# One encoder layer with forgetting attention, RWKV-7 and product-key experts: VectorE in source order in the recurrent part of the second half

## The chip, the core and the metric

The kernel is one program on one core of a Trainium2 chip. The metric is device time in microseconds (us): from the start of the program on the core to its end, median of several executions. Engines are named as the profile names them: PE (TensorE) multiplies matrices, DVE (VectorE) and POOL (GpSimd) do elementwise work, ACT (ScalarE) does activations and copies, SP (SyncE) only issues DMAs. Every engine works through its own queue in the order in which the program was laid out, and an instruction whose inputs are not there yet holds up everything behind it on that engine.

## What is computed

One layer, batch 1, 1024 tokens, width 1024, float32: a combined projection, two token-mixing branches (forgetting attention and RWKV-7), a gated merge with a LayerNorm, and then a product-key mixture of single-neuron experts (PEER) with another LayerNorm. Cut to what matters here:

```python
# branch B, RWKV-7, 8 heads x 64: a recurrence over the tokens
def frame_step(state, inp):
    r_t, w_t, k_t, v_t, kk_t, a_t = inp
    sa = jnp.einsum('bhij,bhj->bhi', state, -kk_t)
    state = (state * w_t[:, :, None, :] + sa[..., None] * (kk_t * a_t)[:, :, None, :]
             + v_t[..., None] * k_t[:, :, None, :])
    return state, jnp.einsum('bhij,bhj->bhi', state, r_t)
# then a group norm per head, a bonus term, and a product with the output gate g

# PEER, per block of 128 tokens xb, 8 heads, 16 experts per head and token
q = (xb @ w_q).reshape(t, 8, 2, 128)
s = jnp.einsum('thpd,hpkd->thpk', q, sub_keys)       # scores against 2 x 128 keys
top_s, top_i = lax.top_k(s, 16)                      # and top 16 of the 256 pair sums: idx, gate
h = jax.nn.gelu(jnp.einsum('thkd,td->thk', u_table[idx], xb))   # gathered rows of u, dot products
return jnp.einsum('thk,thkd->td', gate * h, v_table[idx])
```

## The kernel before

The 1024 tokens go through the front part in two halves of 512 (the loop over `PARTS` in `body`). Each half runs attention (`fox`), then the recurrent branch (`rwkv_half`), then the merge, the first LayerNorm and the expert queries (`merge_half`). After both halves `dense_block` does the experts: three of the eight blocks of 128 tokens as dense products, five by gathered rows.

**Background work.** As soon as the first half has its scores, the experts of its tokens are started beside the second half's front part. This is the queue `g.B` (class `Background`, line 156): for block after block it holds `topk` (line 1266, DVE: maxima, indices, one-hot sums) mixed with `experts_in` (line 1376). `experts_in` gathers, for each of 128 expert slots, one row of the table `u` per token: an indirect DMA that POOL issues (L1389) into one of `GBUF` = 5 buffers `g`; three slots later a DVE instruction (L1394, here called a dot product) multiplies the rows with the tokens `ext` and sums them into a column of `hh`. When the 128 slots of a block are done, a table of gates is loaded, a Gelu and a product follow (L1399 to L1402), and the next block loads its indices (`eidx`, L1380) into the same buffer and starts over. `Background.tick` (line 182) is called by `mm` (line 276) for every matrix product with the product's planned time; the time is added to a credit, and while the credit is positive one step of the queue is written into the program (a dot product counts 1.46 us of credit). So the place of the background work in the source follows the products: so many dot products per us of planned PE time.

**Order.** The program's order on each engine is made when it is built. PE is under a manual schedule (`MANUAL`, line 58): it follows the source. The other engines are ordered by a planner that takes, at every step, the instruction that is first in the source among those whose inputs it believes to be ready. On DVE it may thus set a background instruction ahead of an operation of the recurrence, or the other way round; on the chip the order is then fixed.

**The recurrent part.** `rwkv_half` (line 722) first makes projections (`shifted`, line 750: 24 products, an ACT copy, two DVE instructions L756, L757), then four times `unit(ct)` (line 900), one for each pair of heads. A unit first makes `M` (L918), then inverts a triangular matrix in six levels of three steps, each step a group of products followed by one DVE operation on their result: `x` (L942), `Tm` (L952), `V` (L958); then `At` (L993) and `Q` (L999), and last a loop over the 8 chunks of 64 tokens that carries the state `sigma` (L1010: copied from PSUM by DVE and ACT by turns). Between the steps `wait(...)` (line 904) writes filler work into the source, from a queue `F`: the elementwise preparation `elem` of the next unit (line 819) and projections for the gates (line 760). A group norm and the output gate follow (L1052 to L1080).

**Weights.** Each block of weights `wraw` is split into a high part `wh` (ACT) and a low part `wl` (L295): POOL makes `wl`, except for every eighth block (`g.lo_mod` = 8, line 320), where DVE does.

Of the kernel before, what the change touches and what calls it, by code (L numbers as in the profile page):

```python
# [155 lines left out]
class Background:  # L156


    def __init__(self, tc):
        self.tc = tc  # L160
        self.q, self.done, self.credit, self.rate, self.busy = [], set(), 0.0, 1.0, False
        self.other = None

    def add(self, gen, *tags):
        self.q.append((gen, tags))
# [16 lines left out]
    def tick(self, us):  # L182
        if self.busy or not self.q or (self.other and self.other.busy):
            return
        self.busy = True
        self.credit += us * self.rate
        while self.q and self.credit > 0:
            c = self._step()
            if c is None:
                self.credit = 0.0  # L190
                break
            self.credit -= c
        self.busy = False
# [185 lines left out]
def body(ctx, g):  # L379
# [61 lines left out]
    with ExitStack() as fe:  # L441
        g.X = None
        front_setup(g, fe, order)
        for hf, (t0, n) in enumerate(PARTS):
            g.t0, g.n, g.cols = t0, n, slice(t0, t0 + n)
            with ExitStack() as hx:
                hp = hx.enter_context(tc.tile_pool(name="hp", bufs=1))
                kt = hp.tile([128, 4, n], F32, name="kt")
                if g.X is None:
                    xload(g, hf)  # L450
                g.B.rate = RATEP[0]
                fox(g, hf, g.X)
                g.B.rate = RATEP[1]
                yr = rwkv_half(g, hf, g.X, kt) if g.stop != "fox" else None
                g.xs.close()
                g.X = None
                g.B.rate = RATEP[2]
                if g.stop not in ("fox", "rwkv"):
                    merge_half(g, hf, yr)
# [262 lines left out]
def rwkv_half(g, hf, X, kt):  # L722
# [12 lines left out]
    with ExitStack() as fx:  # L735
# [164 lines left out]
        def unit(ct):  # L900
# [3 lines left out]
            def wait(us):  # L904
                F.fill(WAIT * us)
# [5 lines left out]
            for u in range(0, NC, 4):  # L911
                us = slice(u, u + 4)
                pm = psM.tile([128, 2, 4, 128], F32, name="pm")
                for c in range(4):
                    for e in range(2):
                        mm(g, pm[:, e, c, :], fl(bk[rows[e], u + c, e:e + 2, :]), fl(arv[rows[e], u + c, 0:2, :]), True, True)
                for e in range(2):
                    dve.tensor_mul(M[:, e, us, :], pm[:, e], tb("m1")[:, None, :].to_broadcast([128, 4, 128]))  # L918
                wait(WT[0])
                pt = psM.tile([128, 2, 8, 64], F32, name="pm")  # L920
                for c in range(4):
# [14 lines left out]
            Tm, Vm = None, None  # L936
            for m in range(6):
                px = psS.tile([128, NC, 64], F32, name="s")
                for e, c in items:
                    mm(g, px[rows[e], c, :], LT(e, c), i64[rows[e]] if Tm is None else Tm[rows[e], c, :], True, True)  # L940
                x = cp.tile([128, NC, 64], F32, name="x")
                dve.tensor_mul(x, px, lev[:, m:m + 1, :].to_broadcast([128, NC, 64]))  # L942
                wait(WT[2])
                if m < 5:
                    Tn = cp.tile([128, NC, 64], F32, name="Tm")
                    if Tm is None:
                        dve.tensor_add(Tn, x, i64b)
                    else:
                        pt = psS.tile([128, NC, 64], F32, name="s")
                        for e, c in items:  # L950
                            mm(g, pt[rows[e], c, :], Vm[rows[e], c, :], x[rows[e], c, :], True, True)
                        dve.tensor_add(Tn, pt, Tm)  # L952
                    Tm = Tn
                pv = psS.tile([128, NC, 64], F32, name="s")
                for e, c in items:
                    mm(g, pv[rows[e], c, :], x[rows[e], c, :], i64[rows[e]] if Vm is None else Vm[rows[e], c, :], True, True)
                Vn = cp.tile([128, NC, 64], F32, name="V")
                dve.tensor_add(Vn, pv, i64b if Vm is None else Vm)  # L958
                Vm = Vn
                wait(WT[3])  # L960
                if m == 1:
# [8 lines left out]
            for u in range(0, NC, 8):  # L970
# [8 lines left out]
                for e in range(2):  # L979
                    r = rows[e]  # L980
                    (dve.tensor_copy if e and not SM & 32 else act.copy)(AV[r, e, us, :], pw[r, :, 64:128])
            wait(WT[5])
            pa = psS.tile([128, NC, 64], F32, name="s")
            for e, c in items:
                r = rows[e]
# [11 lines left out]
                mm(g, pq[r, c, :], W_[r, c, :], M[r, e, c, 0:64], True, True)  # L997
            Q = cp.tile([128, NC, 64], F32, name="x")
            dve.tensor_add(Q, pq, arv[:, :, 0, :])  # L999
            wait(WT[6])  # L1000
            py = psS.tile([128, NC, 64], F32, name="s")
            for c in range(NC):
# [4 lines left out]
                    mm(g, pss[r, :], BK[:, e, c, :], AV[:, e, c, :], True, False)  # L1007
                for r in rows:
                    mm(g, pss[r, :], At[r, c, :], g.sigma[r, ct, par, :], False, True)
                (act.copy if c % 2 or SM & 64 else dve.tensor_copy)(g.sigma[:, ct, 1 - par, :], pss)  # L1010
                for e, r in enumerate(rows):
                    mm(g, py[r, c, :], AV[:, e, c, :], M[:, e, c, 0:64], True, False)
                for r in rows:
# [54 lines left out]
        for ct in range(4):  # L1068
# [8 lines left out]
            b = el.tile([128, n], F32, name=("rt", "vt")[ct % 2])  # L1077
            sp.dma_start(b, g.bvd[ct * 128:(ct + 1) * 128, g.t0:g.t0 + g.n])
            pool.tensor_add(y, y, b)
            dve.tensor_mul(y, y, pgs[ct])  # L1080
            if "yr" in g.dbg:
                sp.dma_start(g.dbg["yr"][ct * 128:(ct + 1) * 128, g.t0:g.t0 + g.n], y)
# [765 lines left out]
```

## Time and profile before

| what | us |
|---|---|
| median of 3 executions (3715.09 to 3723.62) | 3722.64 |
| the profiled execution, its own time | 3689.26 |
| span of the profiled execution | 3687.5 |
| DVE busy in the span | 2366.5 (64%) |
| PE busy in the span | 3232.5 (88%) |
| recurrent part of the second half, 1040 to 1600 us of the span | 560 |
| DVE busy in it | 507.46 |
| PE busy in it | 431.97 |

The profiled execution is one execution, 33.4 us below the median of the others. Busy time counts an instruction from its start to its end, also while it is held up by another engine, so "busy" is not "at its peak". A row of the waits view says which instruction ended an idle stretch of an engine, and how much idle time lay before it.

### The profile page before, as it was taken

To read this page: it belongs to the slowest core of one execution; us is meant where nothing else is said; L and a number is where in the kernel's file an instruction comes from. 1 tells how busy PE (TensorE), PEld (TensorE's weight loads), DVE (VectorE), ACT (ScalarE), POOL (GpSimd) and SP (SyncE) were. 2 spreads that over 40 slices of the span, in tenths; PEclk is the share of its full clock that TensorE was granted. 3 is DMA by queue.
4 is the path that set the end of the run, shared out by engine and by line. 5 is a ranking of instruction groups with operands and counts; after the bars stand their busy time and mean duration, and the time that the engine had idled before them with its cause. 6 is when DMAs were issued, how large, how long until landed. Compare 5 with 4: busy or idle time off the path is not lost. (4 is left out here: it accounts for less than half of the span.)

```text
span 3687.5 us, 55563 instructions
## 1 busy us (share of the span) xinstructions
PE 3232.5 (88%) x20656; PEld 2334.0 (63%) x20656; DVE 2366.5 (64%) x5125; ACT 1241.6 (34%) x2530; POOL 2243.2 (61%) x1752
## 2 busy tenths in 40 slices
PE   7899998989987877667868867899998999999998
PEld 5577777875565656546733322587776777777666
DVE  3235423558889998899669955477665767675324
ACT  3443222333443221222234433333333333333333
POOL 2031115326566556677846566688887888886773
PEclk9999999998888777889989989899999999999999
DMA  4121124548877777877869999899999999999994
GB/s 144 52 92 45 45 96 137 189 140 283 262 262 263 243 233 247 295 259 258 309 245 397 395 343 371 337 364 361 385 383 331 392 398 396 394 396 355 403 394 164
DMA packets 338127, 1019.61 MB, mean 277 GB/s; under 512 B 46272, under 2 KB 84928, under 8 KB 336064
## 3 DMA queue, kind: packets, MB, share of 16 engines
q0 software_dynamic: 184320, 671.17, 49.0%
q1 hardware_dynamic: 141424, 324.11, 24.7%
q10 hardware_dynamic: 12112, 20.78, 1.5%
q8 instruction: 162, 2.65, 0.3%
q14 instruction: 109, 0.89, 0.1%
HBM read 960.81 MB, written 55.12 MB: 276 GB/s over the span
## 5 line engine op out<-in xcount | busy, mean ns | idle before, releaser
L1389 POOL DMA_INDIRECT g<-u,eidx x640 | 789.0, 1233 | 397.1 <-DVE hh L1394 114.5
L1394 DVE CUSTOM_DVE_ANT_0 g<-g,ext 128x1024 f32<-128x1024 f32 x640 | 862.5, 1356 | 165.2 <-DMA g<-u,eidx 164.1
L295 POOL TENSOR_TENSOR wl<-wraw,wh 128x1024 fp32r<-128x1024 f32 x131 | 323.7, 2471 | 503.4 <-ACT wh L294 475.6
L1689 POOL DMA_INDIRECT vr<-v,ve x428 | 458.6, 1072 | 193.0 <-issue 99.9
L277 PE MATMUL pg<-vr,win 128*32 128x512 f32 x1712 | 322.4, 633 | 81.9 <-DMA vr<-v,ve 81.1
L277 PE MATMUL b<-xh,uh 128*128 128x384 f32 x1024 | 352.3, 344 | 22.1 <-DVE C L1574 22.0
L277 PE MATMUL b<-xh,ul 128*128 128x384 f32 x1024 | 348.9, 341 | 1.3 <-POOL ul L295 1.1
L277 PE MATMUL b<-xl,uh 128*128 128x384 f32 x1024 | 348.8, 341 | 0.0
L294 ACT CAST wh<-wraw 128x1024 fp32r<-128x1024 f32 x150 | 157.2, 1048 | 505.1 <-PE pj L277 280.2
L277 PE MATMUL v<-vl,ch 128*128 128x512 f32 x768 | 305.9, 398 | 11.2 <-POOL vl L295 11.1
L277 PE MATMUL pj<-xh,wh 128*128 128x512 f32 x624 | 289.9, 465 | 21.1 <-ACT xh L294 7.9
L277 PE MATMUL v<-vh,ch 128*128 128x512 f32 x768 | 303.3, 395 | 0.0
L277 PE MATMUL v<-vh,cl 128*128 128x512 f32 x768 | 301.4, 392 | 0.0
L1689 POOL DMA_INDIRECT C<-v,ve x212 | 225.6, 1064 | 84.8 <-issue 54.4
L294 ACT CAST uh<-uraw 128x512 fp32r<-128x512 f32 x256 | 158.2, 620 | 350.2 <-PE b L277 322.3
L277 PE MATMUL pj<-xh,wl 128*128 128x512 f32 x624 | 262.2, 420 | 4.3 <-POOL wl L295 2.5
L277 PE MATMUL pj<-xl,wh 128*128 128x512 f32 x624 | 263.1, 422 | 2.2 <-DVE xl L295 2.2
L294 ACT CAST vh<-vraw 128x512 fp32r<-128x512 f32 x256 | 157.7, 620 | 217.7 <-PE v L277 182.9
L277 PEld LDWEIGHTS b<-xh,uh 128*128 128x128 f32 x1024 | 194.1, 190 | 55.7 <-DVE C L1574 26.0
L295 POOL TENSOR_TENSOR ul<-uraw,uh 128x512 fp32r<-128x512 f32 x128 | 168.4, 1316 | 88.3 <-ACT uh L294 86.5
L295 DVE TENSOR_TENSOR vl<-vraw,vh 128x512 fp32r<-128x512 f32 x128 | 130.0, 1016 | 143.0 <-ACT vh L294 136.0
L277 PEld LDWEIGHTS b<-xl,uh 128*128 128x128 f32 x1024 | 194.2, 190 | 14.4 <-issue 10.1
(353 smaller groups left out, 6577.5 us busy)
## 6 DMA issues: line engine op xcount, KB each, us to landing
wraw<-w SPq DMA_DIRECT2D x150, 512.0 KB, 3.4
uraw<-ut SPq DMA_DIRECT2D x128, 512.0 KB, 6.6
vraw<-vt SPq DMA_DIRECT2D x128, 512.0 KB, 7.7
cd<-S SPq DMA_DIRECT2D x12, 1344.0 KB, 10.1
C<-cd SPq DMA_DIRECT2D x63, 256.0 KB, 9.2
g<-u,eidx POOLq DMA_INDIRECT x640
gtd<-tmp ACTq DMA_DIRECT2D x32, 256.0 KB, 4.3
g<-gtd SPq DMA_DIRECT2D x32, 256.0 KB, 3.7
```

The source lines that it names most:

```text
L277: g.pe.matmul(o, l, r, start=start, stop=stop_)
L294: g.act.copy(hi, src)
L295: (lo_eng or g.dve).tensor_sub(lo, src, hi.bitcast(F32))
L1389: pool.indirect_dma_start(out=gg, out_offset=None, in_=A["u"], in_offset=bass.IndirectOffsetOnAxis(ap=idx[:, s_:s_ + 1], axis=0))
L1394: dve.tensor_tensor_reduce(out=gg, in0=gg, in1=xt, scale=1.0, scalar=0.0, op0=OP.mult, op1=OP.add, accum_out=hh[:, k:k + 1])
L1689: g.pool.indirect_dma_start(out=place, out_offset=None, in_=g.A["v"], in_offset=bass.IndirectOffsetOnAxis(ap=self.meta[i][1][:, t:t + 1], ...
```

## The change

`Background` gets `hold` and `release`. While it is held, credit is still added up, but no step is written into the source; at the release the steps that the credit allows are written. `unit` holds it around each group of products up to and including the DVE operation that works on them. For the second half alone, DVE follows the source in all of `rwkv_half`, the state copies all go to ACT, and all low parts of weights go to POOL from there to the end of the half (`g.lo_mod` is not set back). In the group norm the last product with the output gate moves into a loop of its own.

```diff
     def tick(self, us):
         if self.busy or not self.q or (self.other and self.other.busy):
             return
+        self.credit += us * self.rate
+        if self.held:
+            return
         self.busy = True
-        self.credit += us * self.rate
...
+    def hold(self):
+        self.held = True
+    def release(self):
+        self.held = False
+        self.tick(0.0)
...
                 g.B.rate = RATEP[1]
+                if hf:
+                    g.lo_mod = 1000
+                    mans(g, MANUAL | {mybir.EngineType.DVE})
                 yr = rwkv_half(g, hf, g.X, kt) if g.stop != "fox" else None
+                mans(g, MANUAL)
...
                 px = psS.tile([128, NC, 64], F32, name="s")
+                g.B.hold()
                 for e, c in items:
                     mm(g, px[rows[e], c, :], LT(e, c), i64[rows[e]] if Tm is None else Tm[rows[e], c, :], True, True)
                 x = cp.tile([128, NC, 64], F32, name="x")
                 dve.tensor_mul(x, px, lev[:, m:m + 1, :].to_broadcast([128, NC, 64]))
+                g.B.release()
                 wait(WT[2])
...
```

The same pair stands around the products and the operation for `M`, for `Tm`, for `V`, and once around `pa`, `At`, `pq` and `Q` together.

```diff
-                (act.copy if c % 2 or SM & 64 else dve.tensor_copy)(g.sigma[:, ct, 1 - par, :], pss)
+                (act.copy if c % 2 or hf else dve.tensor_copy)(g.sigma[:, ct, 1 - par, :], pss)
...
             pool.tensor_add(y, y, b)
+        for ct in range(4):
+            y = yr[:, ct, :]
             dve.tensor_mul(y, y, pgs[ct])
```

In the first half nothing is in the background queue that could run (its scores are not there yet), so there only the last of these edits has an effect on what is written.

## Rows read from the trace of the kernel before

**Rows 1.** Windows view: stretch, its length, busy time (instructions) of each engine, clock.

```profile
1040.00:1600.00 560.00, 431.97 (x4215) 325.00 (x4214) 507.46 (x1115) 139.61 (x212) 366.74 (x271) 0.81 0.77 260
1142.00:1556.00 414.00, 314.76 (x3770) 238.00 (x3769) 371.40 (x876) 86.13 (x137) 255.68 (x196) 0.79 0.76 257
401.00:468.00 67.00, 62.32 (x924) 48.13 (x924) 30.90 (x52) 18.80 (x31) 11.86 (x8) 0.97 0.13 46
1600.00:1740.00 140.00, 97.99 (x421) 76.16 (x420) 133.53 (x235) 33.14 (x43) 100.60 (x61) 0.92 0.74 249
```

**Rows 2.** Waits of PE, 1142 to 1556 us: us in total, times, longest.

```profile
PE s L277 <- DVE x L942: 38.1, 15, 10.1
PE s L277 <- DVE Tm L952: 17.8, 8, 5.5
PE s L277 <- DVE x L999: 15.7, 4, 6.4
```

**Rows 3.** Waits of DVE, 1040 to 1600 us: us in total, times, longest.

```profile
DVE g L1394 <- DMA g<-u,eidx: 24.5, 23, 2.9
DVE sigma L1010 <- PE s L277: 13.5, 8, 3.8
DVE M L918 <- PE pm L277: 4.1, 4, 1.6
```

**Rows 4.** Groups of DVE, 1040 to 1600 us: count | busy, mean ns | idle before.

```profile
L1394 DVE CUSTOM_DVE_ANT_0 g<-g,ext 128x1024 f32<-128x1024 f32 x217 | 291.1, 1351 | 25.0 <-DMA g<-u,eidx 24.5
L295 DVE TENSOR_TENSOR wl<-wraw,wh 128x1024 fp32r<-128x1024 f32 x4 | 4.9, 1218 | 0.0
L1010 DVE COPY sigma<-s 128x64 f32<-128x64 f32 x16 | 3.5, 221 | 13.5 <-PE s L277 13.5
```

**Rows 5.** Groups of ACT, 1142 to 1556 us, and of POOL, 1040 to 1590 us.

```profile
L294 ACT CAST wh<-wraw 128x1024 fp32r<-128x1024 f32 x18 | 18.9, 1048 | 125.2 <-PE pj L277 121.2 <-DVE tv L1290 4.0
L1010 ACT COPY sigma<-s 128x64 f32<-128x64 f32 x16 | 3.4, 211 | 60.9 <-PE s L277 60.8
L871 ACT ACTIVATE ag<-ag,oka,vec 128x512 f32<-128x512 f32 x3 | 2.4, 813 | 11.7 <-DVE kk L866 11.7
...
L295 POOL TENSOR_TENSOR wl<-wraw,wh 128x1024 fp32r<-128x1024 f32 x26 | 65.6, 2522 | 13.1 <-ACT wh L294 12.7
```

**Rows 6.** Timelines of DVE and PE, 1474 to 1506 us: start, length, instruction [idle before].

```profile
1484.42 1.23 DVE L1394 CUSTOM_DVE_ANT_0 g<-g,ext 128x1024 f32<-128x1024 f32 x1 [2.90 <-DMA g<-u,eidx]
1490.14 0.69 DVE L942 TENSOR_TENSOR x<-s,tab 128x512 f32<-128x512 f32 x1
...
1475.40 1.10 PE L277 MATMUL s<-V,x 64*64 64x64 f32 x32
...
1490.89 1.97 PE L277 MATMUL s<-x,V 64*64 64x64 f32 x32 [10.05 <-DVE x L942]
```

**Rows 7.** Timeline of all engines, 1236 to 1262 us.

```profile
1235.69 4.02 DVE L1394 CUSTOM_DVE_ANT_0 g<-g,ext 128x1024 f32<-128x1024 f32 x1
1236.28 2.35 POOL L295 TENSOR_TENSOR wl<-wraw,wh 128x1024 fp32r<-128x1024 f32 x1
1239.92 0.48 PE L277 MATMUL s<-sigma,Tm 64*64 64x64 f32 x4 [3.57 <-DVE sigma L1010]
```

**Rows 8.** Timelines of SP, POOL and DVE, 1136 to 1161 us: a change of block.

```profile
1145.86 0.32 SPq L1380 DMA_DIRECT2D eidx<-seld  x1
...
1148.61 0.96 POOL L1389 DMA_INDIRECT g<-u,eidx  x1 [8.91 <-DVE ti L1299]
...
1153.54 1.22 DVE L1394 CUSTOM_DVE_ANT_0 g<-g,ext 128x1024 f32<-128x1024 f32 x1 [0.78 <-DMA g<-u,eidx]
```

**Rows 9.** Timeline of all engines, 1552 to 1600 us: the group norm.

```profile
1554.12 0.59 ACT L1016 COPY kt<-s 128x512 f32<-128x512 f32 x1 [0.26 <-PE s L277]
1576.00 0.81 ACT L1074 ACTIVATE kt<-kt,vec 128x512 f32<-128x512 f32 x1 [9.61 <-DVE kt L1072]
1580.61 0.79 PE L277 MATMUL a<-xh,wh 128*128 128x512 f32 x1 [0.78 <-DVE kt L1072]
```

More of the change, by code (lines that the diff above doesn't have):

```diff
@@ L161, in __init__ @@
         self.q, self.done, self.credit, self.rate, self.busy = [], set(), 0.0, 1.0, False
-        self.other = None
+        self.other, self.held = None, False
+    def hold(self):
[3 more added lines that the diff above has]
+        self.tick(0.0)
     def add(self, gen, *tags):
@@ L938, in unit @@
                 px = psS.tile([128, NC, 64], F32, name="s")
+                g.B.hold()
                 for e, c in items:
@@ L942, in unit @@
                 dve.tensor_mul(x, px, lev[:, m:m + 1, :].to_broadcast([128, NC, 64]))
+                g.B.release()
                 wait(WT[2])
@@ L949, in unit @@
                         pt = psS.tile([128, NC, 64], F32, name="s")
+                        g.B.hold()
                         for e, c in items:
@@ L952, in unit @@
                         dve.tensor_add(Tn, pt, Tm)
+                        g.B.release()
                     Tm = Tn
                 pv = psS.tile([128, NC, 64], F32, name="s")
+                g.B.hold()
                 for e, c in items:
@@ L958, in unit @@
                 dve.tensor_add(Vn, pv, i64b if Vm is None else Vm)
+                g.B.release()
                 Vm = Vn
@@ L982, in unit @@
             wait(WT[5])
+            g.B.hold()
             pa = psS.tile([128, NC, 64], F32, name="s")
@@ L999, in unit @@
             dve.tensor_add(Q, pq, arv[:, :, 0, :])
+            g.B.release()
             wait(WT[6])
```

## The prediction

> **What bounds the kernel now.** I read the windows view first, in steps of 20 and 100 us, to find the recurrent part of the second half: 1040 to 1600 us of the span. The reader is to see in its row that DVE, and not PE, is the full engine there [rows 1]: DVE is busy 507.5 of 560 us, PE 432.0. The same unit in the first half, with no background, takes 67 us with DVE at 30.9 [rows 1]; here four units take 414 us, 103 each. So the 36 us more per unit are background work on DVE, and what the stage can win without less work on DVE is at most its idle time, 560 - 507.5 = 52.5 us.
>
> Second, the waits of PE. PE waits for `x` 38.1 us, for `Tm` 17.8, for `Q` (written as tile x, L999) 15.7 [rows 2]. It looks like a chain held up by DVE, and this is what the change goes for. But the waits of DVE say what is behind it: its own idle time is mostly dot products that wait for gathered rows (24.5 us, 23 times), then state copies that wait for PE (13.5), then `M` (4.1) [rows 3]. The timeline of one bad place shows both at once [rows 6]: PE has nothing to do for 10.05 us until `x` is there, `x` starts at 1490.14 behind dot products, and the first of these stood 2.90 us waiting for its rows.
>
> The amount of background work in the stage does not change: credit is still counted per planned product, only its place within a few products moves. So this is a sum over DVE's idle time and over the few operations that change engine.
>
> **The change part by part.** Each term is for the stage, in us against before; the numbers in brackets are its bounds.
>
> 1. *State copies to ACT.* 16 copies of 0.221 leave DVE: -3.5. ACT does them in 0.211 each, and it is busy 86 of 414 us there [rows 1, 4, 5]; a copy that comes behind a weight cast waits up to 1.05 [rows 5]. The 13.5 us in which DVE stood at the head of its queue for a state copy go [rows 3]; dot products pass. Part of it comes back, since the chunk loop is bound by PE and ACT and DVE then meets the next unit's `M` early, where it already waits 4.1. I take two thirds: -9 (0 to -13.5).
>
> 2. *Low parts of weights to POOL.* Four in this stage: -4 x 1.218 = -4.9 on DVE [rows 4], +4 x 2.522 = 10.1 on POOL, which is busy 367 of 560 [rows 1, 5]. But a POOL split holds up DVE: a dot product that met one took 4.02 instead of 1.23 [rows 6, 7], 2.8 more, while an unlucky meeting is not certain (the mean dot product is 1.351 [rows 4]). At 1.5 us for each of the four this gives back 6: net +1 (-4.9 to +6.3). A rule speaks against this edit: the Trainium skill, SBUF — State Buffer, section "Who interferes with whom", has it that a DVE instruction with two SBUF inputs and a GpSimd instruction that reads SBUF exclude each other, and the later one blocks fully. By it and the row the whole split would be lost to DVE, 10.1 against 4.9, and this term would be +5 rather than +1; the row agrees with the blocking. The merge and the queries get the same trade for four more blocks; DVE is busy 133.5 of 140 us at first there [rows 1], and I cost it at 0, covered by POOL's split of a block ahead of its use (-3 to +4).
>
> 3. *Chain operation first, dot products behind it.* PE's waits for `x`, `Tm` and `Q` shrink, but that is time only where DVE was idle too. With the hold, dot products come one to three at a time between operations of the chain instead of in rows, so the gathers (five buffers) run further ahead; and while DVE waits for one, PE already works on the next group. Of the 24.5 us of waits for rows [rows 3], 3.7 stand at the two changes of block (0.78 and 2.90 [rows 6, 8]); of the other 20.8 I take 8: -8 (0 to -14). It cannot be more than a part: the filler behind `x` still brings its own ticks, so the credit of 1.7 us (16 products at 0.107 by the plan) and of 1.6 us of filler puts about two dot products between `x` and `Tm` as before.
>
> 4. *Changes of block in source order.* Here the change adds a wait. The first dot product of a new block is the next background step after the gates' product, and DVE now stands at it: from the load of the indices at 1145.86 over the first gather at 1148.61 to the dot product at 1153.54 are 7.7 us [rows 8]. Behind it on DVE are the chain's operations, and PE waits for these. Before, DVE filled this time with maxima of the next block and idled only 0.78 and 2.90 [rows 6, 8]. Two changes lie in the stage: 2 x 7.7 - 3.7 = 11.7 at most, 0 if the gap in the credit (1.46 per step) and chain operations that come in between cover it; half: +6.
>
> 5. *Preparation in source order.* Each of four `elem` has about three DVE operations directly behind an activation (0.81 [rows 5]): up to 12 x 0.81 = 9.8, 0 where dot products stand ahead of them; half: +5.
>
> 6. *Group norm.* From the last copy at 1554.12 to the first product of the merge at 1580.61 pass 26.5 us, 9.61 of them with ACT waiting for one DVE product that stood behind background work [rows 9]. In source order it stands behind the dot product of two matrix products. The product with the gate in a loop of its own keeps DVE from standing at each POOL addition, which it would otherwise do in source order. -5 (-9.6 to +3).
>
> Sum: -3.5 - 9 + 1 - 8 + 6 + 5 - 5 = -13.5 us. On the profiled execution's 3689.26 that is 3675.8. The sum is a difference, and the median of the runs lies 33.4 us above the profiled execution, so the forecast for the median is 3722.64 - 13.5 = 3709. What is won stays won: behind the stage the source places the same work, and DVE still is full up to 1740 [rows 1].
>
> **The rivals.**
>
> *No change.* DVE was 91% busy and its work stays. A planner that passes over what is not ready keeps an engine fuller than the source order does, so terms 1 and 3 may be eaten by 4 and 5. For it: 507.5 of 560. Against it: 13.5 us for state copies that plainly go. Time: terms 1, 2, 4, 5 alone give -3.5 - 9 + 1 + 6 + 5 = -0.5: 3722.
>
> *Slower.* The dot products at the head of DVE's queue wait for rows, and now nothing passes them. Place: every gather that POOL issues behind a split of 2.5 us [rows 5], and the two changes of block. Price: without terms 3 and 4 the sum is -10.5; waits that grow from 1.07 each (24.5 / 23 [rows 3]) to 2.4 are 55 us, 30.7 more: +20, 3743. It decides for slower from 46 us of such waits on, 2.0 each, since -10.5 + 21.5 = +11. For it: DMAs are late already with the planner's order. Against it: 217 dot products in 560 us are one per 2.6 us, twice their length.
>
> *Much faster.* The idle time of PE breaks into short pieces, and with it the granted clock rises. The row before it: after 10.05 us of idle PE ran 32 products in 1.97 us, against 1.10 without such an idle time [rows 6]; the clock is 0.79 in the units here and 0.97 in the first half's [rows 1], between the two levels 1.2 and 2.4 GHz. PE's busy 314.8 us at 0.79 would be some 20% shorter at 0.97. It counts only where PE holds DVE up, in the chunk loop and the group norm; with all terms at their good bounds -3.5 - 13.5 - 4.9 - 14 - 9.6 = -45.5. Time: some 35 us less, 3688.
>
> *It does not do what it says* (the operations still come behind dot products, by the filler's own ticks) is the first rival's time, since then only DVE's total counts.
>
> **How the numbers follow.** A difference of 0.3%, 11 us, is about what a measurement of this kernel can tell from no change. Forecast (11 to 30 us less, 3693 to 3711): 0.36. Much faster: 0.10. No change: 0.32. Slower: 0.22. So faster 0.46, same 0.32, slower 0.22. The predicted time is the forecast's, 3709. The range goes from 3682, which leaves out half of the much faster case (0.05), to 3740, which leaves out about half of the slower one (0.11).
>
> **What would show it.** Term 1: no state copy on DVE in the second half, and no wait of 13.5 for it; where the 9 us went shows in the wait of `M`. Term 2: dot products of 3 to 4 us beside POOL's splits, their mean above 1.351. Term 3: PE's waits for `x` and `Tm` well below 38.1 and 17.8, DVE's for rows below 24.5. Term 4: two gaps of up to 7.7 us on DVE, each ended by the first gather of a block. Term 5: DVE waits that ACT ends. Term 6: less than 26.5 us from the last copy to the merge's first product. The prediction is wrong if DVE's busy time in the stage is not near 500 us, so that the background work did move, or if the gain of the stage is lost again in the merge.

## The result: 1.3% slower, and the profile after

The changed kernel takes 3768.7 us (median of 4 runs, 3765.01 to 3770.3), the kernel before 3720.95 beside it (3715.09 to 3723.62): a ratio of 1.0130, 95% interval 1.0113 to 1.0147. The forecast was 3709, the range ended at 3740. The profiled execution of the changed kernel spans 3763.2 us.

To lay the two executions side by side I cut them at the same events: the end of attention's last product, the first product of unit 0, the last copy of the recurrent part, the first product of the merge, the first product of the one-hot stage (in `dense_block`, behind both halves). Windows view of the kernel before (stretch, length, busy time and instructions of PE, PEld, DVE, ACT, POOL, then PE's clock, DMA share, GB/s): projections and first preparation, the four units, the whole recurrent stretch up to the merge, the merge and the scores.

```profile
1033.60:1142.80 109.20, 91.53 (x361) 70.01 (x360) 101.27 (x169) 42.77 (x61) 80.80 (x54) 0.89 0.79 268
1142.80:1554.10 411.30, 312.07 (x3764) 237.04 (x3763) 369.25 (x867) 84.13 (x132) 254.74 (x195) 0.79 0.76 257
1033.60:1580.60 547.00, 421.43 (x4183) 315.95 (x4182) 494.10 (x1086) 137.16 (x210) 354.19 (x263) 0.81 0.77 260
1580.60:1872.30 291.70, 219.66 (x979) 175.92 (x979) 224.05 (x373) 72.79 (x103) 202.80 (x126) 0.91 0.75 258
```

The same four stretches of the changed kernel:

```profile
1037.80:1150.20 112.40, 87.99 (x354) 68.00 (x354) 88.18 (x130) 39.90 (x59) 80.10 (x51) 0.86 0.67 221
1150.20:1585.30 435.10, 313.07 (x3764) 238.73 (x3764) 388.38 (x884) 88.96 (x151) 269.68 (x201) 0.79 0.76 251
1037.80:1612.20 574.40, 421.29 (x4177) 318.15 (x4177) 496.90 (x1055) 138.34 (x223) 367.69 (x266) 0.80 0.75 246
1612.20:1910.60 298.40, 224.51 (x980) 180.58 (x980) 230.37 (x380) 73.10 (x105) 209.88 (x130) 0.88 0.75 252
```

Read DVE's column against the length. In the whole stretch DVE has the same work, 494.1 and 496.9 us; what grew is its idle time, from 52.9 to 77.5 us, and the stretch with it, from 547.0 to 574.4. Of the 24.6 us of new idle time 16.3 lie ahead of unit 0 (7.9 became 24.2), 4.7 in the units (42.0 to 46.7), 3.6 in the group norm. Ahead of unit 0 the phase itself is only 3.2 us longer, but 13.1 us of DVE work that used to be done there now lie in the units, whose DVE work grew by 19.1. Behind the merge 6.7 us more follow, 6.3 of them DVE work. Together, from attention's end to the one-hot stage: 838.7 to 872.8, 34.1 us more, with DVE work 718.2 to 727.3 and idle time 120.6 to 145.5. Both kernels do 299 dot products in it, 419.0 and 417.4 us. The rest of the span (1815 us before, 1853 after) does not belong to the change: in repeats of both kernels on another chip it took 1816.0 (e0_before_again) and 1811.5 (e8_after_again).

Waits of DVE in the changed kernel, 1040 to 1612 us (us in total, times, longest), the answer to [rows 3]:

```profile
DVE g L1420 <- DMA g<-u,eidx: 34.4, 24, 8.9
DVE rt L770 <- ACT tmp L768: 6.2, 2, 5.3
DVE M L933 <- PE pm L287: 6.1, 3, 5.3
DVE lora L770 <- ACT tmp L768: 4.0, 1, 4.0
```

The state copies' 13.5 us are gone. Waits for rows grew by 9.9 us with almost the same count: the longest is 8.9 instead of 2.9. The growth lies at the two changes of block (below), not in the other waits for rows. New are operations that wait for ACT. PE's waits in the units, 1150 to 1588 us (answer to [rows 2]), and ahead of them, 1040 to 1150 us:

```profile
PE s L287 <- DVE x L959: 49.7, 18, 11.0
PE s L287 <- DVE Tm L971: 26.9, 8, 6.8
PE pm L939 <- DVE M L933: 19.1, 4, 12.2
PE s L287 <- DVE x L1022: 5.1, 4, 1.3
...
PE pj L287 <- POOL wl L305: 11.6, 1, 11.6
PE s L287 <- ACT tmp L818: 10.8, 2, 8.5
```

PE waits longer for `x` (38.1 before) and `Tm` (17.8), though these now stand ahead of the dot products; only `Q` (15.7 to 5.1) is better off. The groups of DVE, ACT and POOL (answers to [rows 4, 5]):

```profile
L1420 DVE CUSTOM_DVE_ANT_0 g<-g,ext 128x1024 f32<-128x1024 f32 x212 | 285.9, 1365 | 34.5 <-DMA g<-u,eidx 34.4
...
L1034 ACT COPY sigma<-s 128x64 f32<-128x64 f32 x32 | 6.8, 212 | 57.8 <-PE s L287 56.0 <-ACT sigma L1034 1.6
...
L305 POOL TENSOR_TENSOR wl<-wraw,wh 128x1024 fp32r<-128x1024 f32 x30 | 76.4, 2546 | 25.4 <-ACT wh L304 25.1
```

**A change of block** (timelines of SP, POOL, DVE and PE of the changed kernel, 1162 to 1180 us; answer to [rows 8]):

```profile
1164.35 0.33 SPq L1425 DMA_DIRECT2D eidx<-gated  x1
...
1167.60 0.29 DVE L1427 TENSOR_TENSOR hh<-hh,eidx 128x128 f32<-128x128 f32 x1 [1.02 <-DMA eidx<-gated]
...
1167.92 0.32 SPq L1406 DMA_DIRECT2D eidx<-seld  x1
...
1171.42 0.96 POOL L1415 DMA_INDIRECT g<-u,eidx  x1 [9.98 <-DMA eidx<-seld]
...
1175.68 1.22 DVE L1420 CUSTOM_DVE_ANT_0 g<-g,ext 128x1024 f32<-128x1024 f32 x1 [7.79 <-DMA g<-u,eidx]
...
1176.83 1.28 DVE L933 TENSOR_TENSOR M<-pm,tab 128x512 f32<-128x512 f32 x2
...
1178.26 0.37 PE L939 MATMUL pm<-base,bkh 64*128 64x64 f32 x2 [12.23 <-DVE M L933]
```

From the load of the indices at 1167.92 to the dot product at 1175.68 are 7.76 us, as before; but now DVE stands at that dot product for 7.79 us, `M` stands behind it, and PE behind `M` for 12.23. The second change costs 2.31 us for the product with the gates and 8.91 for the first dot product:

```profile
1495.49 0.96 DVE L1427 TENSOR_TENSOR hh<-hh,eidx 128x128 f32<-128x128 f32 x1 [2.31 <-ACT hh L1426]
1505.36 1.23 DVE L1420 CUSTOM_DVE_ANT_0 g<-g,ext 128x1024 f32<-128x1024 f32 x1 [8.91 <-DMA g<-u,eidx]
```

In the kernel before the first dot products of the two blocks waited 0.78 [rows 8] and 1.47 us, and the second ones 2.83 and 2.90 [rows 6]:

```profile
1159.05 1.22 DVE L1394 CUSTOM_DVE_ANT_0 g<-g,ext 128x1024 f32<-128x1024 f32 x1 [2.83 <-DMA g<-u,eidx]
1479.69 1.23 DVE L1394 CUSTOM_DVE_ANT_0 g<-g,ext 128x1024 f32<-128x1024 f32 x1 [1.47 <-DMA g<-u,eidx]
```

In the changed kernel the second ones wait 0 and 0.26. So the first two dot products of the new blocks went from 8.0 to 17.0 us of waiting, and all other waits for rows from 16.5 to 17.4.

**The phase of the projections** (timelines of ACT, POOL and PE of the changed kernel, 1120 to 1137 us):

```profile
1124.28 1.05 ACT L304 CAST wh<-wraw 128x1024 fp32r<-128x1024 f32 x1 [3.79 <-PE pj L287]
...
1124.74 1.75 POOL L1415 DMA_INDIRECT g<-u,eidx  x1 [3.30 <-DVE hh L1420]
1127.84 1.64 POOL L1415 DMA_INDIRECT g<-u,eidx  x1 [1.35 <-DVE hh L1420]
...
1133.97 2.51 POOL L305 TENSOR_TENSOR wl<-wraw,wh 128x1024 fp32r<-128x1024 f32 x1
...
1136.53 0.80 PE L287 MATMUL pj<-xh,wl 128*128 128x512 f32 x1 [11.64 <-POOL wl L305]
```

This one I had not foreseen. The gathers on POOL wait for buffers that late dot products free (`DVE hh`). A low part of weights stands behind five gathers in POOL's queue; ACT had its input ready at 1125.33, POOL starts at 1133.97, and PE has nothing to do for 11.64 us. A late DVE thus comes back to PE over POOL's queue.

### The profile page after: what moved, and what is told of

Read it like the earlier page. It is cut to its first block, busy times and chain, and to the rows that moved or that the text cites. A ratio compares the mean times of both kernels' runs of the same rounds, so it can differ in the third digit from the quotient of the medians.

```text
span 3763.2 us, 55577 instructions
## 1 busy us (share of the span) xinstructions
PE 3236.2 (86%) x20656; PEld 2346.7 (62%) x20656; DVE 2363.6 (63%) x5101; ACT 1240.1 (33%) x2545; POOL 2271.0 (60%) x1760
## 3 DMA queue, kind: packets, MB, share of 16 engines
q0 software_dynamic: 184320, 671.17, 48.6%
q1 hardware_dynamic: 141424, 324.11, 24.6%
## 5 line engine op out<-in xcount | busy, mean ns | idle before, releaser
L305 POOL TENSOR_TENSOR wl<-wraw,wh 128x1024 fp32r<-128x1024 f32 x139 | 343.0, 2467 | 510.4 <-ACT wh L304 484.0
L287 PE MATMUL pg<-vr,win 128*32 128x512 f32 x1712 | 311.2, 646 | 82.4 <-DMA vr<-v,ve 74.3
L287 PEld LDWEIGHTS v<-ab 128*128 128x128 f32 x768 | 113.0, 219 | 167.9 <-issue 103.5
```

The costliest lines, as they stand in the source:

```text
L287: g.pe.matmul(o, l, r, start=start, stop=stop_)
L305: (lo_eng or g.dve).tensor_sub(lo, src, hi.bitcast(F32))
```

## Experiments

Kernels of one group ran on one chip beside the kernel before, which took 3692.49 us (e0 to e3), 3727.05 (e4 to e7), 3693.79 (e8 to e11), 3698.33 (e12 to e15) and 3691.06 (e16, e17). All ratios are to the kernel before on that chip; "stretch" is from attention's end to the merge in the profiled execution, DVE's idle time is its length less DVE's busy time.

| kernel | ratio [95%] | stretch | DVE busy | idle |
|---|---|---|---|---|
| before / after | 1.0130 [1.0113, 1.0147] | 547.0 / 574.4 | 494.1 / 496.9 | 52.9 / 77.5 |
| e0_before_again | 1.0002 [0.9978, 1.0026] | 542.6 | 494.0 | 48.6 |
| e1_planner_order | 1.0023 [1.0002, 1.0045] | 545.7 | 500.2 | 45.5 |
| e2_source_order_alone | 1.0126 [1.0086, 1.0166] | 594.5 | 506.0 | 88.5 |
| e3_from_units | 1.0077 [1.0055, 1.0099] | 569.2 | 490.5 | 78.7 |
| e4_pause | 1.0081 [1.0055, 1.0107] | 586.9 | 501.6 | 85.3 |
| e5_units_pause | 1.0056 [1.0035, 1.0078] | 570.6 | 496.5 | 74.1 |
| e6_sigma_only | 1.0008 [0.9992, 1.0023] | 542.5 | 492.9 | 49.6 |
| e7_no_lo | 1.0012 [0.9995, 1.0029] | 562.0 | 499.7 | 62.3 |
| e8_after_again | 1.0107 [1.0085, 1.0129] | 576.5 | 496.5 | 80.0 |
| e9_prep_only | 1.0065 [1.0040, 1.0089] | 553.2 | 497.3 | 55.9 |
| e10_source_lo8 | 1.0081 [1.0057, 1.0106] | 569.8 | 497.1 | 72.7 |
| e11_units_pause_lo8 | 1.0072 [1.0047, 1.0096] | 570.0 | 499.8 | 70.2 |
| e12_source_no_hold | 1.0113 [1.0087, 1.0140] | 580.7 | 495.5 | 85.2 |
| e13_half_before | 0.9751 [0.9724, 0.9778] | 469.8 | 348.9 | 120.9 |
| e14_half_after | 0.9755 [0.9732, 0.9779] | 510.6 | 386.3 | 124.3 |
| e15_rate | 1.0142 [1.0118, 1.0166] | 498.8 | 452.0 | 46.8 |
| e16_rate_shift | 0.9993 [0.9973, 1.0014] | 492.6 | 450.4 | 42.2 |
| e17_rate_small | 0.9987 [0.9966, 1.0007] | 524.2 | 481.0 | 43.2 |

The idle time is that of one execution: e1 and e7 differ by 16.8 us in it and by 0.1% in the ratio, so a difference of that size in this column decides nothing by itself.

**Which edit: the order or the rest.** First the kernel before unaltered, then the change without its order, then the order alone:

```diff
# e1_planner_order: the changed kernel, less one line
-                    mans(g, MANUAL | {mybir.EngineType.DVE})
# e2_source_order_alone: the kernel before, with that line (and its end) alone
+                if hf:
+                    mans(g, MANUAL | {mybir.EngineType.DVE})
                 yr = rwkv_half(g, hf, g.X, kt) if g.stop != "fox" else None
+                mans(g, MANUAL)
```

> The kernel before, once more, for a second profile of it: the first one (3689 us) lies some 30 us under the other executions. The source-order theory, by which the loss lies in the recurrent part: time 3715 to 3724, and the stretch from the first product of unit 0 in the second half to the end of the queries' scores as in the first profile, 719 us (1142.8 to 1861.7), within 5 us; what the first profile had less than a usual execution lies behind it, in the one-hot part and the experts (1800 us in the first profile, about 1830 here). The rival that part of the loss lies in the experts: this stretch is 1800 us again.

> The changed kernel with one line taken out: DVE stays in the planner's order in the second half. Hold and release, the state copies on ACT, the low parts of weights on POOL and the group norm's second loop stay. Source-order theory: the loss goes, ratio to the kernel before 0.995 to 1.003, PE's waits of 12.2 and 11.6 us at the change of block and for the low part of a weight go. Rival, that the edits around it (more work on POOL, copies on ACT, dot products bunched by the hold) are the cause: it stays at 1.01 or above.

> The kernel before with that one line added: DVE in source order in the recurrent part of the second half, no hold, state copies on both engines, low parts as before. Source-order theory: slower than the kernel before by as much as the changed kernel or more, ratio 1.013 to 1.03, since chain operations now also stand behind the dot products of their own products. Rival (the other edits are the cause): 0.997 to 1.003.

With the planner's order all the other edits together give 1.0023; the order alone gives 1.0126, as much as the whole change. So the order is the cause; the other edits together cost 0.23% (0.02 to 0.45%) and gain nothing.

**Where: ahead of the units or in them.**

```diff
# e3_from_units: source order only from unit 0 on (in rwkv_half; not in body)
         F.drain()
+        if hf:
+            mans(g, MANUAL | {mybir.EngineType.DVE})
         for ct in range(4):
# e9_prep_only: source order only ahead of unit 0
+        if hf:
+            mans(g, MANUAL)
         for ct in range(4):
```

> The changed kernel with the source order beginning only at unit 0: projections, the first preparation and the first five gates stay in the planner's order. Source-order theory with two places: the loss ahead of unit 0 goes (the first products of M come 3 to 9 us sooner), the changes of block stay: ratio 1.006 to 1.011. If all of the loss came from the changes of block: 1.012 as the changed kernel. If all of it came from the projections: 1.000.

> The changed kernel again, unaltered, so that the next kernels stand beside it on one chip: 1.011 to 1.015 of the kernel before.

> The changed kernel with VectorE in source order only until the first unit (projections, first operands, gates); the planner orders VectorE in the units and the group norm. The converse of e3_from_units. Nothing is left out. If the two places add up, 1.013 less 1.0077 - 1.0023 of the units leaves 1.006 to 1.009, and VectorE's idle time ahead of the first unit is 23 to 25 us as in the changed kernel (7.9 in the kernel before) with some 45 us in the units and behind, as in e1_planner_order's 31. Rival (what the order loses ahead of the units comes back in the planner's units, because VectorE is caught up there): 1.001 to 1.004.

Over e1's 1.0023, e3 costs 0.54% and e9 0.42%; the sum of both and e1, 1.012, is within the interval of the whole in e8 (1.0107). Both places cost, by the medians about equally; e9's interval still touches e1's. The place in e9's profile was not as expected: 12.4 us idle ahead of unit 0 instead of 23 to 25. But there PE takes the first products of unit 0 with 311 products done instead of some 360 (87.6 us after attention's end, with 75.2 us of DVE work done), so that the two phases don't hold the same work and this expectation is not tested.

**The changes of block.** The background waits out the start of a block, and its other dot products give the credit back:

```diff
# e4_pause (changed kernel) and e5_units_pause (e3); g.pz is 8.0 in the second half's recurrent part
         gg = rows.pop(k)
+        if k == 0 and g.pz:
+            yield 6.0
...
-        yield 1.46
+        yield 1.46 - g.pz / 128
...
     act.activation(hh, hh, AF.Gelu)
+    if g.pz:
+        yield 2.0
     dve.tensor_mul(hh, hh, gate)
```

> The changed kernel, in which the background generator pauses at a change of block: 6.0 us of credit ahead of the first dot product of a block and 2.0 us between GELU and the product with the gates, given back by the other dot products of the block (each is charged 1.46 - 8/128 us). Nothing is left out. Theory Q (in source order the products at a change of block stand at the head of VectorE's queue and wait there for index load, gather and GELU; 20.0 us of waiting in the profile of the changed kernel: 1.0 + 7.8 at the first change, 2.3 + 8.9 at the second): VectorE's idle time between the attention's end and the merge falls from 77.5 us to 60 to 65 us, and the ratio from 1.013 to 1.007 to 1.010. Rival P (the loss is in the phase of the projections and in the order as a whole; the waits at the changes are taken from time in which VectorE would have waited anyway): 1.011 to 1.014.

> Source order only from unit 0 on, with the same pauses at the changes of block. Nothing is left out. Theory Q: 1.008 without the pauses becomes 1.002 to 1.005; VectorE's idle time in the stretch falls from 78.7 us to some 60 us. Rival P: 1.007 to 1.009.

The long gaps do go. Waits of DVE for rows in e4, 1033 to 1610 us:

```profile
DVE g L1425 <- DMA g<-u,eidx: 31.1, 21, 5.0
```

The longest is 5.0 instead of 8.9. But the idle time of the stretch does not fall as Theory Q has it: 85.3 us in e4 (77.5 in the changed kernel, 60 to 65 expected) and 74.1 in e5 (78.7 in e3, some 60 expected). Other waits grew instead, such as DVE's for PE at `M`, 10.3 us in e4 against 6.1. The ratios, 1.0081 and 1.0056, went the way of Theory Q, but against 1.0130 and 1.0107 for the changed kernel and 1.0077 for e3 they were measured on other chips, and e5's interval overlaps e3's. On the chip of e3 (1.0077, no pauses) e11 below has the pauses (and the low parts shared as before) and takes 1.0072, which speaks for the low end. So the changes of block cost something between nothing and 0.5%; the runs don't settle it.

**Low parts of the weights.** `g.lo_mod = 1000` is taken out of e1 (e7), of the changed kernel (e10), and of e5 (e11, all three suspects undone at once):

```diff
                 if hf:
-                    g.lo_mod = 1000
```

> The changed kernel in the planner's order (as e1_planner_order), with the low parts of the weights shared as in the kernel before (every eighth on VectorE). Nothing is left out. In e1_planner_order the dot products took 1406 ns on the mean against 1357 ns in the kernel before, 10.7 us over 221 of them, and 4 low parts of 1.22 us left VectorE. If the low parts on GpSimd are what makes the dot products longer: the mean falls to some 1360 ns and the ratio from 1.0023 to 1.000 to 1.001. If the length of the dot products comes from elsewhere: 1.002 to 1.004.

> The changed kernel with the low parts of the weights shared as before (every eighth on VectorE). Nothing is left out. If GpSimd's extra low parts (2.5 us each, in one queue with the gathers) are a cause of their own: idle time ahead of the first unit falls from 24 to some 17 us and the ratio to 1.009 to 1.011. If with source order the phase of the projections loses its 16 us anyway (e2_source_order_alone lost 15 with the shares of before): 1.012 to 1.014.

> All three suspects undone at once: source order only from unit 0 on, pauses at the changes of block, low parts of the weights shared as before. Nothing is left out. If the phase of the projections, the changes of block and the low parts make up the loss: 1.000 to 1.003. If source order costs in the units by itself, away from the changes (products that wait for rows or for the holds): 1.005 to 1.007, as e5_units_pause.

Three pairs differ in this edit alone. With all low parts on POOL the mean dot product (1030 to 1600 us) is longer by 28 ns in the planner's order (1378 in e7, 1406 in e1), by 13 in source order (1345 in e10, 1358 in e8) and by 11 in the third pair (1401 in e11, 1412 in e5), which is 2 to 6 us over the stretch. But among the kernels that share the low parts as before the mean runs from 1337 (e2) to 1401 (e11), so other things move it more than this edit. The total moves by 0.1% (e1 against e7) and 0.26% (e8 against e10), and the other way in the third pair (e5 1.0056, e11 1.0072); no pair is clear of its intervals, and the first and third stand on two chips each. In e10 the idle time ahead of unit 0 stayed at 23.9 us, so that part of the expectation fell. In e11 all three suspects are undone and 0.72% stayed: the second of its two theories, by which source order costs in the units by itself. What is left shows in the windows ahead of unit 0, of e7 (planner's order throughout) and of e11 (planner's order ahead of unit 0, source order behind), with the same shares:

```profile
1032.80:1145.50 112.70, 90.44 (x360) 69.03 (x358) 106.07 (x194) 42.87 (x62) 83.27 (x54) 0.89 0.80 270
```

```profile
1035.10:1148.90 113.80, 92.37 (x363) 70.81 (x362) 95.32 (x145) 41.29 (x60) 85.18 (x54) 0.88 0.78 264
```

The phase takes the same time, but the planner gets 49 more instructions and 10.8 us more DVE work into it, since it may reach into what the source places in the units: among them the maxima and indices of the next block, of which one group in e7 is

```profile
L1322 DVE FIND_INDEX8 ti<-tv,s 128x8 uint32<-128x128 f32 x7 | 2.0, 279 | 0.0
```

and which e11 and the changed kernel don't have in that phase at all. Source order costs not only where an instruction stands at the head of the queue and waits; it also takes away the work that used to fill every other hole, on both sides of the line where it begins.

**Is chain-first worth anything?** The changed kernel without its holds:

```diff
# e12_source_no_hold
     def hold(self):
-        self.held = True
+        pass
```

> The changed kernel without the holds: VectorE still in source order, and the dot products stand ahead of the chain's own operations again, where their credit falls due. Nothing is left out. The prediction's third term (chain first: some 45 chain operations per unit, each up to a dot product earlier, the gain taken at 8 us): 1.011 with the holds becomes 1.013 to 1.016 without, and TensorE's waits for x, Tm and M grow by over 10 us. Rival (VectorE is full, so that the order among its operations only moves the waits; the holds cost VectorE waits of their own ahead of M): 1.009 to 1.012.

1.0113 against 1.0107 in e8, on another chip. PE's waits in the units, first of e12 (1153 to 1594 us), then of e8 (1150 to 1588 us):

```profile
PE s L287 <- DVE x L959: 61.9, 19, 12.2
PE pm L939 <- DVE M L933: 21.0, 6, 9.6
PE s L287 <- DVE x L1022: 11.8, 4, 3.6
```

```profile
PE s L287 <- DVE x L959: 52.9, 20, 11.3
PE pm L939 <- DVE M L933: 18.2, 4, 11.4
PE s L287 <- DVE x L1022: 4.8, 4, 1.3
```

The holds do what they say in part: PE waits 9.0 us less for `x`, 7.0 less for `Q`, 2.8 less for `M`, but 8.5 more for two other operations of the chain (`Tm`, L965 and L1016: 12.5 in e12, 21.0 in e8). DVE's idle time in the stretch falls from 85.2 to 80.0 us, its waits for rows in the units from 37.8 to 32.8. The total did not follow beyond what can be told. A wait of PE is not time, as long as DVE is busy in it.

**Is it DVE that sets the length?** Half of each dot product's columns left out, in both kernels; then fewer dot products in the stretch:

```diff
# e13_half_before (kernel before), e14_half_after (changed kernel)
-        dve.tensor_tensor_reduce(out=gg, in0=gg, in1=xt, scale=1.0, scalar=0.0, op0=OP.mult, op1=OP.add, accum_out=hh[:, k:k + 1])
+        dve.tensor_tensor_reduce(out=gg[:, 0:512], in0=gg[:, 0:512], in1=xt[:, 0:512], scale=1.0, scalar=0.0, op0=OP.mult, op1=OP.add, accum_out=hh[:, k:k + 1])
# e6_sigma_only: the kernel before, with the state copies on ACT
-                (act.copy if c % 2 or SM & 64 else dve.tensor_copy)(g.sigma[:, ct, 1 - par, :], pss)
+                (act.copy if c % 2 or hf else dve.tensor_copy)(g.sigma[:, ct, 1 - par, :], pss)
# e15_rate: e6, and
-                g.B.rate = RATEP[1]
+                g.B.rate = RATEP[1] * (0.85 if hf else 1)
# e16_rate_shift: e15, and 1.2 instead of 0.9 in merge_half of the second half; e17_rate_small: 0.93 and 1.05
```

> The kernel before with dot products over 512 of the 1024 columns (the other half of each product is left out; the gathers are as before). Stands beside e14_half_after. If VectorE's work sets the stretch, it gets shorter by most of what the dot products lose there: 213 of 1.35 us become some 0.7 us, 130 us at most; bounded by the chain and by the gathers, 40 to 100 us of the stretch and 0.95 to 0.98 in all. If the chain's latency sets it: within 15 us of before in the stretch.

> The changed kernel with the same halved dot products (the other half is left out). Theory F (what source order costs is idle time of an engine that is full: every hole is lost work): with VectorE half free the holes are made good, and the difference to e13_half_before falls from 40 us to 10 to 20 us, which are the two changes of block. Theory L (source order lengthens the chain itself, by waits at the head of the queue and late operands): the difference stays at 30 to 50 us.

> The kernel before with one edit: all copies of the state on ScalarE in the second half. Nothing is left out. If VectorE's busy and waiting time is what sets the length of the stretch, 16 copies of 0.22 us and 9 to 13 us of waits for sums of the state go: 8 to 14 us, ratio 0.996 to 0.998. If the planner had nothing else to put there, or gives the time back as other waits: 0.999 to 1.001.

> The kernel before with the copies of the state on ScalarE and the background's rate in the recurrent part of the second half at 0.85 instead of 1. Nothing is left out; some 32 of 213 dot products (1.35 us each, 43 us of VectorE) move out of the stretch to the parts behind. If VectorE is the bound of the stretch and has room behind it: 0.990 to 0.997. If what is moved costs as much behind (the stages behind, with 224 us of 292 busy on VectorE): 0.999 to 1.003.

> As e15_rate (copies of the state on ScalarE, background at 0.85 in the recurrent part of the second half), and the background at 1.2 instead of 0.9 in the merge and the routing scores behind, so that the dot products that were moved are done before the one-hot stage asks for them. Nothing is left out. In e15_rate the routing scores ended 39 us earlier than in e0_before_again, and the one-hot stage then waited 98.4 us for its operands behind the dot products left over. If the scores have room on VectorE (60 us idle of 290): the 39 us less 10 to 25 us that some 28 dot products add there, no wait of over 20 us in the one-hot stage: 0.992 to 0.997. If the scores grow by as much as the stretch lost: 0.999 to 1.002; if the one-hot stage still waits: above 1.005.

> The same shift at half the size: 0.93 in the recurrent part, 1.05 behind. Nothing is left out. With room in the scores: 0.995 to 0.998; without: 0.999 to 1.002.

Halving the dot products makes the kernel before 2.5% faster (e13), though all gathers are still there: DVE's work sets the time. With DVE half free the two orders come out alike: 0.9751 and 0.9755, medians 3601.64 and 3608.24. The 37 us between e8 and its kernel before shrink to 7. At the start of the one-hot stage 18.5 us are left (1800.1 and 1818.6 us into the profiled executions) where e0 and e8 show 51.5 (1862.4 and 1913.9). By the time this is Theory F: most of what the order loses is the time of a full engine.

The stretch alone does not say so: it takes 469.8 us in e13 and 510.6 in e14, 40.8 more, as Theory L has it, with PE waiting 29.8 us for `x` instead of 8.5. It does not hold the same work, though. In e13 the planner took 278 more DVE instructions into the part ahead of it (1380 against 1102 in e0), so that attention ends at 1048.2 us instead of 1028.5, and e13's stretch has 37.5 us less DVE work than e14's; the idle time is the same, 120.9 and 124.3 us. That is why I compare from the start of the program. Some of the loss, up to 18.5 us in the front part, is a longer chain. And one rival stands: DVE waits 80.0 us for rows in the stretch of e13 and 75.6 in e14, so gathers may have become the limit, and such a limit would hide a longer chain too.

e15 and e16 look from the other side; there the gathers move along with the dot products, so that they do not tell the one from the other. Windows of e0, from attention's end to the merge and from there to the one-hot stage, then of e16:

```profile
1028.50:1571.10 542.60, 410.49 (x4183) 308.48 (x4182) 494.03 (x1086) 137.27 (x210) 358.30 (x263) 0.83 0.79 263
1571.10:1862.40 291.30, 224.30 (x980) 180.42 (x980) 223.93 (x373) 72.81 (x103) 202.12 (x126) 0.88 0.76 258
```

```profile
1035.40:1528.00 492.60, 402.31 (x4182) 301.92 (x4180) 450.36 (x972) 140.27 (x225) 324.19 (x234) 0.86 0.77 258
1528.00:1862.30 334.30, 232.67 (x979) 185.51 (x979) 265.46 (x472) 73.31 (x104) 244.23 (x154) 0.83 0.79 270
```

43.7 us of DVE work moved out shorten the stretch by 50.0; 41.5 us moved into the merge and the scores lengthen them by 43.0, though DVE is idle there for 67 of 291 us. The total is the same, 0.9993. In e15, where the work moved and the rate behind was not raised, the one-hot stage stood still for it (waits of PE, 1823 to 2350 us; 4.1 us in e0):

```profile
PE v L277 <- DVE ab L1470: 98.4, 14, 62.7
```

e6 missed on the gain's side: no wait for state copies is left, 3.5 us of copies left DVE, and the ratio is 1.0008, the idle time 49.6 (52.9 and 48.6 in the two profiles of the kernel before). The time came back as other waits, such as this one at the group norm (waits of DVE in e6, 1033 to 1610 us; 2.0 us in e0):

```profile
DVE kt L1052 <- PE s L277: 7.5, 2, 7.0
```

None of the complete kernels beats the kernel before by more than can be told; e17, at 0.9987 [0.9966, 1.0007], comes nearest.

## Why the prediction was wrong

What held: DVE is the full engine, its work in the stretch does not change (494.1 and 496.9 us), and only its idle time is to be won or lost. The argument even named the way it went, in the rival of no change: a planner that passes over what is not ready keeps an engine fuller. What failed is the step from waits to time: terms 1 and 3 counted waits that go as time won, and terms 4 to 6 costed source order at single waits, with nothing for the work that the planner had pulled into the holes. All that the order was to do, terms 3 to 6, adds up to -2 us; the order alone cost 46 us (e2, 3738.5 against 3692.49). Terms 1 and 2 add up to -11.5; the kernel with all edits but the order was 8.8 us slower (e1, 3701.31). With -13.5 expected and +34.1 found up to the one-hot stage, step by step:

1. *State copies to ACT, -3.5 - 9.* Right in what is seen: no copy on DVE, the 13.5 us of waits gone. Wrong as time: alone it gives 1.0008 (e6). I had let a third come back; nearly all did, in part as waits of the next operations in the same chain (the group norm's `kt`, 7.5 us in e6).

2. *Low parts to POOL, +1.* The size is small, and the sign open: 0.1% and 0.26% slower in two pairs, 0.16% faster in the third, none beyond the intervals. The +5 that followed from the Trainium skill's "Who interferes with whom" (SBUF — State Buffer) is not told apart from +1 by these runs. The row agrees with it that one instruction stands still beside the other, but not that it is the later one: the dot product of [rows 7] began 0.59 us ahead of the split, and it was the dot product that took longer. What I left out is POOL's queue: a low part stands behind gathers that wait for DVE, and PE lost 11.64 us at one such place.

3. *Chain first, -8.* This term failed. The holds shorten some of PE's waits (e12 against e8), take 5 us of DVE's waits for rows, and bring no time that can be told. Against the kernel before, the waits for rows away from the changes of block did not fall by 8 but stayed (16.5 and 17.4 us). I also read one of them wrongly: the 2.90 that I took off as a first dot product is the second one of its block, and the first waited 1.47. DVE's wait for PE at `M` grew (5.3 us at the longest, 1.6 before [rows 3]); the holds are not its cause, since it is 7.3 without them (e12).

4. *Changes of block, +6.* The mechanism was there as described, and larger: 1.02 + 7.79 and 2.31 + 8.91 us, 20.0 against 2.3 for the same instructions before (12.3 more with the second dot products of both blocks), where 11.7 more was the upper bound. Yet the units as a whole idle only 4.7 us more: the 13.5 us of state copies went at the same time. I had left out the product ahead of it, which waits for the gates (1.02) and for the Gelu (2.31). What of it is time stays open (e4, e5).

5. *Preparation in source order, +5 (at most +9.8).* Mis-sized, and the largest miss by place: 16.3 of the 24.6 us of new idle time lie ahead of unit 0. I counted operations of `elem` behind activations of 0.81 us. But source order starts with `rwkv_half`, so that the projections are under it too; there DVE waits 5.3 us for `rt` and 4.0 for `lora` at one go, and no maxima of the next block are at hand any more. Source order in that part alone costs 0.42% over e1, some 15 us (e9).

6. *Group norm, -5.* Nothing came of it. Timeline of ACT and PE in the changed kernel, answer to [rows 9]:

```profile
1585.28 0.59 ACT L1040 COPY kt<-s 128x512 f32<-128x512 f32 x1 [0.25 <-issue]
...
1607.68 0.81 ACT L1098 ACTIVATE kt<-kt,vec 128x512 f32<-128x512 f32 x1 [5.67 <-DVE kt L1096]
...
1612.18 0.80 PE L287 MATMUL a<-xh,wh 128*128 128x512 f32 x1 [2.24 <-DVE kt L1096]
```

From the last copy to the merge 26.9 us pass, 26.5 before; the one wait of 9.61 became several.

The rival that ended slower named waits for rows as its mechanism and 46 us of them as the point from which it decides. They reached 34.4, 1.43 each. So the time of that rival, 3743, came nearer for a reason that it does not give. (Its sum was off by one: without terms 3 and 4 the terms add up to -11.5, not -10.5, which gives 3742 and 47 us.) The clock of the much faster rival did not rise: 0.79 in the units, before and after. The reason found is the first rival's, with a larger price: source order as such keeps DVE idle, here in every part of the stretch, and an idle DVE is time because DVE is full (e13 and e14, with the rival named there).

Open are the shares of the single places inside the units, where DVE's waits for PE at `M` come from, and the 6.3 us of DVE work by which the merge and the scores grew.

## What to carry to other kernels

On an engine that is busy nine tenths of a stretch, another order can win at most its idle time, and waits of the other engines are no measure of it: ask for each idle piece what else was ready to fill it. Fixing the source order takes the fillers away everywhere, also ahead of where it starts, so price it by the work that the planner had pulled forward and not only by the instructions that will wait. Before forecasting a gain from a wait that goes, look for the next wait in the same chain, and follow a late engine through the queues that wait for its buffers (here POOL's gathers, and the weights behind them).

## What the runs showed of the hardware that was not expected

A dot product stands still beside a low part on POOL also when it began first. Between 1030 and 1600 us of the kernel before, ten of POOL's 27 low parts met a dot product that then took 2.6 to 4.8 us instead of 1.2; in four of the ten the dot product had begun first, as in [rows 7]. That four more low parts on POOL make the mean dot product longer is seen in all three pairs (11 to 28 ns), but within a spread of 1337 to 1401 ns among kernels without them. Putting the state copies on one engine, ACT, at 212 ns each cost nothing that can be told (1.0008 in e6): in the changed kernel 32 copies took 6.8 us, and only 1.6 us of ACT's waits ahead of them are for ACT's own copies.
